# Hybrid decoder block on one Trainium2 core: first-row scores in one matmul for all heads, output-projection tiles held behind the last PV, merged high and low parts in the up projection

## The chip, the core and the metric

The kernel runs on one core of one Trainium2 chip. The metric is the device time of one execution in microseconds (us). A core has five engines that this text names as the profile does: PE (matrix multiply), PEld (its weight loads), DVE (elementwise), ACT (activation functions and copies), POOL (GpSimd; here it mostly issues adding DMAs) and SP (it only issues DMAs). Every engine works through its own queue in order. Matmul results go to PSUM, eight banks of 512 fp32 columns; the rest lies in SBUF.

## What is computed

A decoder block for 512 rows of width 1024, all in fp32; `x` is (1, 512, 1024):

```python
h = rmsnorm(x, norm_attn_g)
q, k, v, u_pool, u_gate = split(h @ w_in)        # 8 heads, two 64-wide score sets each, rope on q and k
w = softmax(s[:, :, 0]) - lam * softmax(s[:, :, 1])   # causal, in blocks of 128 rows
o = rmsnorm(w @ v, subln_g) * (1 - lam_init)
merged = sigmoid(g_A) * o + sigmoid(g_P) * pool(u_pool)   # gates u_gate, windows 2, 4, 8, 16
x = x + merged @ w_out
z = square(relu(rmsnorm(x, norm_mlp_g) @ w_up))  # 1024 -> 4096
x = x + z @ w_down                               # 4096 -> 1024
return rmsnorm(x, final_norm_g)
```

## The kernel before

**Numbers in two parts.** Each fp32 operand of a large matmul is split into a high part `hi` (rounded to fp32r) and a low part `lo` (the rest). A product is then three matmuls: hi by hi, hi by lo, lo by hi. A weight is split by `split_w`: ACT casts it (L112), DVE subtracts (L113).

**Attention (L372 to L545).** For each head `h`, `qk(h)` projects and rotates q and k, and `attn(h)` takes four row tiles `i`. The scores of a tile are, for each of the two sets `c`, two matmuls with the low and the high part of k (L406, L407). In the first tile, `i == 0`, heads 0 to 5 take another way (`whole`, L400): one matmul of 256 columns for each `c` gives both parts, and a DVE add (L402) and the following L408 bring them together. Heads 6 and 7 take the plain way with 128 columns. Then come softmax, transposes (L422), casts and subtracts of the weights `wt` (L424, L425), and PV (L430), twelve matmuls into bank 7. The row norm of the head's output follows: `sq`, a matmul with ones (`ss`, L445) into the same bank 7, and `rsqrt` on it: Ln, Exp, Square on ACT (L204, L205, L206), then two DVE instructions (L207, L208). L204 and L207 read `ss`, so bank 7 is free for the next head's PV only when L207 is done. Between these steps PE works on fillers: projections of gates and pools, dealt out by `LAG`. After every fifth filler, `gt` of a group of two heads goes through a sigmoid (L521), with an ACT table load ahead of it and one after it (L524), and `merge` makes the merged heads (L490 to L507), with matmuls `pp` (L499 to L503).

**Output projection (L622 to L656).** Its left half, `po0`, has a bank for each of four row tiles `t`. The weights come in four pieces `kk`; piece `kk` serves `k = 2kk, 2kk + 1`. The matmuls of `k = 4` are held behind the last PV (`state["pv"]`). The right half, `po1`, follows tile by tile. The last weight piece of `po1` reuses the buffer of the last piece of `po0`. A finished tile is added to x (`x1_add`, L604, and a Square, L578). Then each tile gets its row scale, is normed (`h2`, L655) and transposed (`h2T`, L663), and its parts are written to `gab` (L675, L676).

**MLP (L683 on).** The hidden width is done in four blocks `q`, each an `up(q)` and a `down(q)`. Each is a 2 by 2 block product with seven products instead of eight (forms A11, A12, S1, S2, S3, A22, S4 of the activations, kept in `gab` and `gss`). In `up`, a product is 48 matmuls of 256 columns: for each of two banks `i` and two halves `p`, four `k` with `hi` by the activations' high part (L802), four with `hi` by their low part (L805), four with `lo` by the high part (L808). A11, S2, S3 and A22 pile up in the same two banks `ma`, and after each of the first three its state is read: `keep` copies it (ACT, L830), `join` adds it (DVE, L834). `z_of` applies Relu and Square (L840, L841), `sub` and `zsplit` (L785, L783, L772, L775) make the forms of z for `down`, whose products are 24 matmuls of 512 columns (L895, L897, L898) and end in `to_x1` (L915). Weight forms for S1, S2 and A22 are made in place by adding DMAs (`plus`, L704, on POOL's queue), then split.

**Order.** Tile's scheduler moves instructions within each engine's queue by a time line of its own. `after(later, earlier)` gives it one more rule of order; it is not a wait of its own.

Of the kernel before, what the change touches and what calls it, by code (L numbers as in the profile page):

```python
# [51 lines left out]
def block_kernel(ctx, tc, xT, x_tok, gains, pos, consts, w_in, w_v, w_pool, w_out, w_up, w_dn, out):  # L52
# [334 lines left out]
    def attn(h, qs, kk):  # L387
        ks, kz = (kk[:, i] for i in range(2))
        wt = wt_all
        for i in range(NT):  # L390
            N = (i + 1) * P
            qsl = slice(i * P, i * P + P)
            pr = tmp(f"p{i}", f"p{h}_{i}", (P, 2, N), bufs=1)
            st = tmp("st", f"st{h}_{i}", (P, 6), bufs=3)
            whole = i == 0 and h < 6
            if whole:

                both = sbk(f"s{h}_0").rearrange("p (c k n) -> p c k n", c=2, k=2)
                for c in range(2):
                    T.matmul(both[:, c], lhsT=qs[:, c, qsl], rhs=kk[:, :, c, :P], start=c == 0, stop=True, skip_group_check=True)  # L400
                diag = mask[:, S - P :].rearrange("p (o n) -> p o n", o=1).to_broadcast([P, 2, P])
                V.tensor_tensor(out=pr, in0=both[:, :, 0], in1=diag, op=ALU.add)  # L402
            for c in range(2):
                if not whole:
                    s_ = sbk(f"s{h}_{i}_{c}")
                    T.matmul(s_[:, :N], lhsT=qs[:, c, qsl], rhs=ks[:, c, :N], start=True, stop=False)  # L406
                    T.matmul(s_[:, :N], lhsT=qs[:, c, qsl], rhs=kz[:, c, :N], start=False, stop=True)  # L407
# [12 lines left out]
            t_ = tbk(f"t{h}_{i}")  # L420
            for j in range(i + 1):
                T.transpose(out=t_[:, j * P : j * P + P], in_=pr[:, 0, j * P : j * P + P], identity=ident)  # L422
            tv = t_[:, :N].rearrange("p (j q) -> p j q", q=P)
            state["wt"] = A.copy(out=wt[:, 0, : i + 1, qsl], in_=tv)  # L424
            V.tensor_tensor(out=wt[:, 1, : i + 1, qsl], in0=tv, in1=f(wt)[:, 0, : i + 1, qsl], op=ALU.subtract)  # L425
# [181 lines left out]
    def forms_h2(forms, x):  # L607

        w, u, a11, a12 = (h_[:, i, :, x] for h_ in (hw, h2f) for i in range(2))
        for form in forms:  # L610
            ins = None
            if form in (S2, S4):
                ins = V.scalar_tensor_tensor(out=w, in0=w, scalar=-1.0, in1=a11 if form == S2 else a12, op0=ALU.mult, op1=ALU.subtract)
            elif form == S3:
                ins = V.tensor_tensor(out=u, in0=a11, in1=u, op=ALU.subtract)
            if form in (S3, S4):
                after(ins, state[form - 1])
            hi, lo = (g_[:, :, x] for g_ in gf[form])
            A.copy(out=hi, in_=u if form == S3 else w)
            state[form] = V.tensor_tensor(out=lo, in0=u if form == S3 else w, in1=f(hi), op=ALU.subtract)  # L620

    po = [bank(t, f"po0_{t}") for t in range(NT)]  # L622
    for kk in range(4):
        w = get_w(w_out[0, kk], f"o0_{kk}", V if kk else "dma", state["scaled"] if kk > 1 else None)
        for k in (2 * kk, 2 * kk + 1):
            for t in range(NT):
                m, _ = mm_rows(po[t], t, k, w, k == 0, k == NK - 1)
                if k == 4:
                    after(m, state["pv"])
    for t in range(NT):  # L630
        nc.sync.dma_start(out=x1[:, t, :], in_=x_tok[t])
# [5 lines left out]
    ws = []  # L637
    for kk in range(4):
        raw, hi, lo = load_w(w_out[1, kk], f"o1_{kk}")
        cast = split_w(raw, hi, lo, eng=V)  # L640
        ws.append((hi, lo))
    for ins in sq0:
        after(ins, cast)
    for t in range(NT):
        a_ = bank(4 + t, f"po1_{t}")
        for k in range(NK):
            m, end = mm_rows(a_, t, k, ws[k // 2], k == 0, k == NK - 1)
            if t > 1 and k == 0:
# [22 lines left out]
        if t == 3:  # L671
            forms_h2((S3,), slice(0, HS))
        for b in range(t // 2, 2):
            hi, lo = (gab[b][:, t // 2, i, :, sl] for i in range(2))
            A.copy(out=hi, in_=pv[b])  # L675
            part = V.tensor_tensor(out=lo, in0=pv[b], in1=f(hi), op=ALU.subtract)  # L676
# [12 lines left out]
    def weights(src, q, nm, order):  # L689
# [16 lines left out]
        def parts(rs, b, hold=None, add=None):  # L706
# [4 lines left out]
            for c in range(2):  # L711
# [51 lines left out]
    def halves(r):  # L763
        return [r[:, 2 * i : 2 * i + 2, :] for i in range(2)]

    def bank_view(pa):
        return [pa[i].rearrange("p (a t) -> p a t", a=2) for i in range(2)]

    def zsplit(q, form, r):

# [4 lines left out]
        lo = V.tensor_tensor(out=z[:, 1], in0=r, in1=f(z[:, 0]), op=ALU.subtract)  # L775
        if q == 0 and form == A11:
            after(lo, state["join"])

    def sub(o, x, y, neg=False):

        o, x, y = (R[i] for i in (o, x, y))
        if neg:
            V.scalar_tensor_tensor(out=o, in0=x, scalar=-1.0, in1=y, op0=ALU.mult, op1=ALU.subtract)  # L783
        else:
            V.tensor_tensor(out=o, in0=x, in1=y, op=ALU.subtract)  # L785

    def up(q):

        W = weights(w_up, q, "u", (A11, A12, S1, S2, S3, A22, S4) if q == 0 else (A11, S1, S2, S3, A22, A12, S4))

        def product(form, name, onto=None):
            w, pa = next(W), onto or [acc(f"u{name}{q}_{i}") for i in range(2)]
            rh, rl = gf[form]
            first.append(None)
            for i in range(2):
                hi, lo = w[i]
                for p in range(2):
                    begin = None
                    a_ = pa[i][:, p * HS : p * HS + HS]
# [26 lines left out]
            return pa  # L826

        def keep(pa, r):
            for a_, r_ in zip(bank_view(pa), halves(r)):
                state["keep"] = A.copy(out=r_, in_=a_)  # L830

        def join(pa, r, hold=None):
            for a_, r_ in zip(bank_view(pa), halves(r)):
                state["join"] = V.tensor_tensor(out=r_, in0=a_, in1=r_, op=ALU.add)  # L834
# [33 lines left out]
        zhi["z21"] = z_of(R[3], 1.0, ma)
# [183 lines left out]
```

## Time and profile before

| | |
|---|---|
| median of 3 runs | 671.15 us (670.84 to 671.32) |
| the profiled execution | 670.35 us |
| its span, first to last instruction | 668.6 us |
| granted PE clock | 0.998 |
| busy: PE, DVE, ACT, POOL | 99%, 80%, 70%, 14% |
| HBM read | 106.07 MB, 162 GB/s over the span |

The span is 1.75 us shorter than the time of the execution; what lies around it is outside the profile. Busy PE counts matmuls that overlap in a pipeline, so two starts are closer together than the length shown for one; the pace is read from starts. `out<-in` gives the tile written and those read. A bracket at the end of a row is idle time before it and what ended that. For windows, the columns are the stretch, its length, then busy time and number of instructions of each engine, granted clock, DMA share and GB/s.

### The profile page before, as it was taken

How to read it: one execution, taken by the hardware profiler on the slowest of the kernel's cores; microseconds unless marked ns; L12 is line 12 of the kernel's file. 1: busy time of each engine (PE TensorE's matmuls, PEld its weight loads, DVE VectorE, ACT ScalarE, POOL GpSimd, SP SyncE). 2: the span in 40 equal slices, each digit the busy share in tenths (PEclk: the TensorE clock that was granted, in tenths of full speed). 3: DMA queues.
4: the chain of work that ended last, by engine and by line, in shares of the span. 5: the costliest groups of instructions: out<-in, count | busy, mean ns of one | idle time of the engine just before them, and what ended most of it. 6: DMA issues, size and time to landing. Idle time of an engine off the chain costs nothing.

```text
span 668.6 us, 9970 instructions
## 1 busy us (share of the span) xinstructions
PE 659.8 (99%) x3668; PEld 576.7 (86%) x3668; DVE 531.6 (80%) x903; ACT 469.0 (70%) x756; POOL 92.5 (14%) x115
## 2 busy tenths in 40 slices
PE   9999999999999999999999999999999999999995
PEld 7888888888888888888789988999889998899884
DVE  6855977799879987895588998659993699657995
ACT  8465577988878689886577974368733695266875
POOL 3001110031113111300202030302102021210120
PEclk9999999999999999999999999999999999999999
DMA  8516465354445365554877495876949588584863
GB/s 319 166 61 179 125 151 139 69 146 96 120 109 140 113 140 112 126 186 161 269 203 137 156 235 166 184 212 139 243 168 205 173 179 257 121 200 136 211 126 127
DMA packets 32738, 108.83 MB, mean 163 GB/s; under 512 B 4016, under 2 KB 4912, under 8 KB 32688
## 3 DMA queue, kind: packets, MB, share of 16 engines
q0 software_dynamic: 10512, 38.28, 31.9%
q1 hardware_dynamic: 21744, 69.38, 29.6%
q8 instruction: 29, 0.48, 0.3%
q10 hardware_dynamic: 432, 0.52, 0.2%
q14 instruction: 21, 0.17, 0.1%
HBM read 106.07 MB, written 2.10 MB: 162 GB/s over the span
## 4 chain that ended last, share of the span: by engine, by line
PE 98%; DVE 0%; DMA 0%; ACT 0%; issue 0%; SPq 0%
PE um L805 8%; PE um L808 8%; PE um L802 8%; PE dm L897 8%; PE dm L895 8%; PE dm L898 8%; PE v L237 2%; PE o L430 2%; PE ga L137 2%; PE gp L133 2%; PE gp L134 2%; PE gp L137 2%; PE k L134 2%; PE ga L134 2%; PE k L133 2%; PE k L137 2%
## 5 line engine op out<-in xcount | busy, mean ns | idle before, releaser
L897 PE MATMUL dm<-wh_dt,z 128*128 128x512 f32 (+1 forms) x128 | 49.5, 386 | 0.0
L898 PE MATMUL dm<-wl_dt,z 128*128 128x512 f32 (+1 forms) x128 | 49.4, 386 | 0.0
L895 PE MATMUL dm<-wh_dt,z 128*128 128x512 f32 (+1 forms) x128 | 49.0, 387 | 0.0
L805 PE MATMUL um<-gss,wh_ut 128*128 128x256 f32 x192 | 48.2, 283 | 0.0
L802 PE MATMUL um<-gss,wh_ut 128*128 128x256 f32 x192 | 48.0, 283 | 0.0
L915 DVE TENSOR_TENSOR x<-x,dm 128x512 f32<-128x512 f32 x48 | 32.6, 682 | 16.7 <-PE dm L898 16.7
L112 ACT CAST wh_ut<-wga_uNone 128x1024 fp32r<-128x1024 f32 x24 | 24.9, 1052 | 29.1 <-PE dm L897 15.0
L112 ACT CAST wh_ub<-wr_u 128x1024 fp32r<-128x1024 f32 x24 | 25.1, 1050 | 25.6 <-PE um L805 11.1
L413 ACT ACTIVATE p<-p,st 128x128 f32<-128x128 f32 (+3 forms) x64 | 35.7, 559 | 5.9 <-DVE st L408 5.7
L113 DVE TENSOR_TENSOR wl_ut<-wga_uNone,wh_ut 128x1024 fp32r<-128x1024 f32 x24 | 29.0, 1222 | 12.6 <-ACT wh_ut L112 12.6
L897 PE MATMUL dm<-wh_db,z 128*128 128x512 f32 x96 | 37.2, 389 | 0.0
L898 PE MATMUL dm<-wl_db,z 128*128 128x512 f32 x96 | 37.2, 389 | 0.0
L805 PEld LDWEIGHTS um<-gss,wh_ut 128*128 128x128 f32 x192 | 36.9, 192 | 0.0
L802 PEld LDWEIGHTS um<-gss,wh_ut 128*128 128x128 f32 x192 | 36.8, 192 | 0.0
L895 PE MATMUL dm<-wh_db,z 128*128 128x512 f32 x96 | 35.7, 389 | 0.0
L113 DVE TENSOR_TENSOR wl_ub<-wr_u,wh_ub 128x1024 fp32r<-128x1024 f32 x24 | 29.1, 1220 | 8.3 <-ACT wh_ub L112 8.3
L704 POOL DMA_DIRECT2D wga_dNone<-w_dn x16 | 13.9, 871 | 152.2 <-DVE wl_dt L113 152.2
L775 DVE TENSOR_TENSOR z<-rawz,z 128x1024 fp32r<-128x1024 f32 x28 | 33.6, 1219 | 1.5 <-ACT z L772 1.4
L112 ACT CAST wh_dt<-wga_dNone 128x1024 fp32r<-128x1024 f32 x24 | 24.8, 1047 | 11.6 <-issue 7.5
L805 PE MATMUL um<-gab,wh_ub 128*128 128x256 f32 x128 | 32.5, 283 | 0.0
L802 PE MATMUL um<-gab,wh_ub 128*128 128x256 f32 x128 | 32.4, 283 | 0.0
L704 POOL DMA_DIRECT2D wga_uNone<-w_up x18 | 15.6, 864 | 115.6 <-DVE wl_ut L113 99.2
(326 smaller groups left out, 2185.3 us busy)
## 6 DMA issues: line engine op xcount, KB each, us to landing
wr_u<-w_up SPq DMA_DIRECT2D x24, 512.0 KB, 5.5
wr_d<-w_dn SPq DMA_DIRECT2D x24, 512.0 KB, 4.1
wga_uNone<-w_up POOLq DMA_DIRECT2D x18, 512.0 KB, 7.1
wga_dNone<-w_dn POOLq DMA_DIRECT2D x16, 512.0 KB, 5.5
wr_k<-w_in SPq DMA_DIRECT2D x8, 512.0 KB, 3.3
wr_ga<-w_in SPq DMA_DIRECT2D x8, 512.0 KB, 3.4
wr_gp<-w_in SPq DMA_DIRECT2D x8, 512.0 KB, 4.1
wl_ga<-w_in POOLq DMA_DIRECT2D x8, 512.0 KB, 5.6
```

Of the source, the lines that this page charges most:

```text
L112: ins = A.copy(out=hi[:, sl], in_=raw[:, sl])
L113: state["low"] = (eng or G).tensor_tensor(out=lo[:, sl], in0=raw[:, sl], in1=f(hi)[:, sl], op=ALU.subtract)
L134: T.matmul(acc, lhsT=hi[:, c], rhs=rl[k], start=False, stop=False)
L137: T.matmul(acc, lhsT=lo[:, c], rhs=rh[:, k, :], start=False, stop=k == NK - 1)
L413: A.activation(out=pr[:, c, :N], in_=pr[:, c, :N], func=AF.Exp, scale=-1.0, bias=st[:, c : c + 1], accum_out=st[:, 2 + c : 3 + c])
L775: lo = V.tensor_tensor(out=z[:, 1], in0=r, in1=f(z[:, 0]), op=ALU.subtract)
L802: m = T.matmul(a_, lhsT=hi[:, c], rhs=rh[:, k, :], start=p + k == 0 and onto is None, stop=False, skip_group_check=True)
L805: T.matmul(a_, lhsT=hi[:, c], rhs=rl[:, k, :], start=False, stop=False, skip_group_check=True)
L808: m = T.matmul(a_, lhsT=lo[:, c], rhs=rh[:, k, :], start=False, stop=k == 3, skip_group_check=True)
L895: m = T.matmul(a_, lhsT=zh, rhs=hi[:, sl], start=p == 0 and start, stop=False, skip_group_check=True)
L897: T.matmul(a_, lhsT=zl, rhs=hi[:, sl], start=False, stop=False, skip_group_check=True)
L898: end = T.matmul(a_, lhsT=zh, rhs=lo[:, sl], start=False, stop=p == 3, skip_group_check=True)
```

## The change

Four edits:

1. `whole` holds for all eight heads: heads 6 and 7 take the way of L400 too.
2. The matmuls of `k = 0` for tiles 0 and 2 of `po0` are held behind the last PV as well; those of `k = 4` of `po1`'s tile 1 are held behind the end of `po0`'s tile 3.
3. The last weight piece of `po1` is cast and subtracted in two halves of 512 columns.
4. In `up(q)` for q = 1, 2, 3 the products A11, S2, S3 and A22 are `wide`: the activations' high and low parts lie side by side (`gab`, `gss` are laid out `[..., 4, 2, HS]`), and one matmul of 512 columns does what L802 and L805 did. The `lo` matmuls stay at 256 columns. The result has its two halves in one bank, and a product has four banks instead of two. So `keep` becomes an ACT copy and a DVE add for each of four banks, `join` two DVE adds for each, and A22's `z_of` goes through `keep` first. The rotation of banks is set for each q. In `up(3)`, the weight of A12 is loaded and split ahead of A22's. Some `after` rules are added for weight casts and for `sub`.

```diff
-            whole = i == 0 and h < 6
+            whole = i == 0 and h < 8
...
-                if k == 4:
+                if k == 4 or k == 0 and t % 2 == 0:
                     after(m, state["pv"])
...
-        cast = split_w(raw, hi, lo, eng=V)
+        for sl in (slice(0, 512), slice(512, 1024)) if kk == 3 else (slice(0, 1024),):
+            cast = split_w(raw, hi, lo, sl, eng=V)
...
+            elif t == 1 and k == 4:
+                after(m, state["po0", NT - 1])
...
+            if nm == "u" and q == 3 and form == A22:
+                b21 = parts(raw(2), "b21")
...
+                    if wide:
+                        ab = pa[2 * i + p]
+                        a_ = ab[:, :HS]
...
+                        if wide:
+                            m = T.matmul(ab, lhsT=hi[:, c], rhs=both[:, k].rearrange("p a t -> p (a t)"), start=k == 0 and onto is None, stop=False, skip_group_check=True)
+                            first[-1] = first[-1] or m
+                            continue
...
         def keep(pa, r):
+            if len(pa) == 4:
+                for i, ab in enumerate(map(split_view, pa)):
+                    state["kept", i] = A.copy(out=r[:, i, :], in_=ab[:, 1])
+                    V.tensor_tensor(out=r[:, i, :], in0=ab[:, 0], in1=r[:, i, :], op=ALU.add)
+                return
...
         def join(pa, r, hold=None):
+            if len(pa) == 4:
+                for i, ab in enumerate(map(split_view, pa)):
+                    for j in range(2):
+                        ins = V.tensor_tensor(out=r[:, i, :], in0=ab[:, j], in1=r[:, i, :], op=ALU.add)
+                        state["joined", i] = ins
+                return
...
+            if pa and len(pa) == 4:
+                keep(pa, r)
+                pa = None
...
+        wide = q > 0
+        if wide:
+            x, y, z = ((0, 1), (6, 7), (4, 5)) if q % 2 else ((4, 5), (6, 7), (0, 1))
+            acc.ids, acc.n = x + y + z + x + y + x + z, 0
+        ma = product(A11, "m1", wide=wide)
...
+        product(S2, "m6", onto=ma, wide=wide)
...
+        product(S3, "m7", onto=ma, wide=wide)
...
+        product(A22, "m4", onto=ma, wide=wide)
```

With the edits the scheduler also places other instructions anew. Three places follow.

The first is ACT's queue at the row norm of head 6, near the end of attention: `y_2499` (in the change `y_2497`) is head 6's norm, `ss` its sum, `t_3` the last score tile of head 7, and `g` the gates of the last group. Before:

```order
L112 CAST wh_o_3_3081<-wr_o_3_3079 128x1024
L424 CAST wt<-t_2_2701 128x3x128
L204 ACTIVATE y_2499<-ss_2497,eps 128x512
L205 ACTIVATE y_2499<-y_2499 128x512
L206 ACTIVATE sqo_2489<-y_2499 128x512
L424 CAST wt<-t_3_2723 128x4x128
L521 ACT_TABLE_LOAD
L521 ACTIVATE g_2761<-g_2761 128x2048
L524 ACT_TABLE_LOAD
```

In the change:

```order
L112 CAST wh_o_3_3077<-wr_o_3_3075 128x1024
L204 ACTIVATE y_2497<-ss_2495,eps 128x512
L424 CAST wt<-t_3_2719 128x4x128
L521 ACT_TABLE_LOAD
L521 ACTIVATE g_2757<-g_2757 128x2048
L524 ACT_TABLE_LOAD
L205 ACTIVATE y_2497<-y_2497 128x512
L206 ACTIVATE sqo_2487<-y_2497 128x512
```

The cast of `t_3`, both table loads and the sigmoid moved from behind L206 to between L204 and L205. On PE, 4 transposes and 26 matmuls of 512 columns stand between `ss` of head 6 and the PV of head 7 before; in the change it is 4 transposes and 18 matmuls.

The second is PE's queue where `po0` ends and `po1` first needs its last weight piece; `po_0_2984` to `po_3_2987` (in the change `po_0_2980` to `po_3_2983`) are the tiles of `po0`, the others those of `po1`, and `wl_o_3_3152` (`wl_o_3_3148`) is the low part of the last piece. Before:

```order
L600 MATMUL po_3_2987<-wh_o_3_3081,vl 128x512
L600 MATMUL po_1_3204<-wh_o_1_3139,vl 128x512
L598 MATMUL po_1_3204<-wh_o_2_3145,vh 128x512
L599 MATMUL po_1_3204<-wl_o_2_3146,vh 128x512
L600 MATMUL po_1_3204<-wh_o_2_3145,vl 128x512
L598 MATMUL po_1_3204<-wh_o_2_3145,vh 128x512
L599 MATMUL po_1_3204<-wl_o_2_3146,vh 128x512
L600 MATMUL po_1_3204<-wh_o_2_3145,vl 128x512
L598 MATMUL po_0_3155<-wh_o_3_3151,vh 128x512
L598 MATMUL po_1_3204<-wh_o_3_3151,vh 128x512
L599 MATMUL po_0_3155<-wl_o_3_3152,vh 128x512
```

In the change (two rows more at the head):

```order
L600 MATMUL po_0_2980<-wh_o_3_3077,vl 128x512
L600 MATMUL po_1_2981<-wh_o_3_3077,vl 128x512
L600 MATMUL po_2_2982<-wh_o_3_3077,vl 128x512
L600 MATMUL po_3_2983<-wh_o_3_3077,vl 128x512
L598 MATMUL po_1_3202<-wh_o_2_3141,vh 128x512
L599 MATMUL po_1_3202<-wl_o_2_3142,vh 128x512
L600 MATMUL po_1_3202<-wh_o_2_3141,vl 128x512
L598 MATMUL po_1_3202<-wh_o_2_3141,vh 128x512
L599 MATMUL po_1_3202<-wl_o_2_3142,vh 128x512
L600 MATMUL po_1_3202<-wh_o_2_3141,vl 128x512
L598 MATMUL po_0_3153<-wh_o_3_3147,vh 128x512
L598 MATMUL po_1_3202<-wh_o_3_3147,vh 128x512
```

The four tiles of `po0` now end in four successive matmuls, 12 matmuls ahead of the first use of the last low part; before, tiles 0, 1 and 2 ended 8, 6 and 3 matmuls ahead of tile 3's end, the first row shown. On DVE the four `x1_add` of these tiles stand ahead of the last piece's subtract in both programs.

The third is DVE's queue at the parts of the first two normed tiles; `h2T_0_3237` (`h2T_0_3235`) is the second tile's transpose for A11, whose parts go to `gab_2978` (`gab_2974`), and `h` is a normed tile. Before:

```order
L676 TENSOR_TENSOR gab_2978<-h2T_0_3188,gab_2978 128x4x128
L676 TENSOR_TENSOR gab_2979<-h2T_1_3193,gab_2979 128x4x128
L676 TENSOR_TENSOR gab_2978<-h2T_0_3237,gab_2978 128x4x128
L591 SCALAR_TENSOR_TENSOR st_2983<-st_2983 128x1
L676 TENSOR_TENSOR gab_2979<-h2T_1_3242,gab_2979 128x4x128
L604 TENSOR_TENSOR x_2974<-po_3_3305,x_2974 128x512
L592 SCALAR_TENSOR_TENSOR st_2983<-st_2983 128x1
L655 SCALAR_TENSOR_TENSOR h_2976<-x_2974,st_2983,rawz 128x1024
```

In the change:

```order
L679 TENSOR_TENSOR gab_2974<-h2T_0_3186,gab_2974 128x4x128
L679 TENSOR_TENSOR gab_2975<-h2T_1_3191,gab_2975 128x4x128
L591 SCALAR_TENSOR_TENSOR st_2979<-st_2979 128x1
L592 SCALAR_TENSOR_TENSOR st_2979<-st_2979 128x1
L658 SCALAR_TENSOR_TENSOR h_2972<-x_2970,st_2979,rawz 128x1024
L679 TENSOR_TENSOR gab_2974<-h2T_0_3235,gab_2974 128x4x128
L604 TENSOR_TENSOR x_2970<-po_3_3303,x_2970 128x512
L679 TENSOR_TENSOR gab_2975<-h2T_1_3240,gab_2975 128x4x128
```

The normed third tile (L658) moved ahead of the second tile's first subtract. On PE, seven matmuls of `po1` stand between the second tile's transposes and the first matmul of `up(0)` before, and three in the change.

More of the change, by code (lines that the diff above doesn't have):

```diff
@@ L560, in block_kernel @@
     h2f = zf("h2f", F32)
-    gab = [big.tile([P, j, 2, 4, HS], F32R, tag=t_, name=f"gab{j}") for j, t_ in ((1, "s1a"), (2, "s4"))]
-    gss = [big.tile([P, 2, 2, 4, HS], F32R, tag=f"s{i}", name=f"gss{i}") for i in (2, 3)]
+    gab = [big.tile([P, j, 4, 2, HS], F32R, tag=t_, name=f"gab{j}") for j, t_ in ((1, "s1a"), (2, "s4"))]
+    gss = [big.tile([P, 2, 4, 2, HS], F32R, tag=f"s{i}", name=f"gss{i}") for i in (2, 3)]
     gf = {}
     for form, g_, j in ((A11, gab[0], 0), (A12, gab[1], 0), (A22, gab[1], 1), (S1, gss[0], 0), (S2, gss[0], 1), (S3, gss[1], 0), (S4, gss[1], 1)):
-        gf[form] = (g_[:, j, 0], g_[:, j, 1])
+        gf[form] = (g_[:, j, :, 0], g_[:, j, :, 1], g_[:, j])
     rawz = bk.tile([P, 5, 4, HS], F32, name="rawz")
@@ L617, in forms_h2 @@
                 after(ins, state[form - 1])
-            hi, lo = (g_[:, :, x] for g_ in gf[form])
+            hi, lo = (g_[:, :, x] for g_ in gf[form][:2])
             A.copy(out=hi, in_=u if form == S3 else w)
@@ L626, in block_kernel @@
             for t in range(NT):
-                m, _ = mm_rows(po[t], t, k, w, k == 0, k == NK - 1)
-                if k == 4:
+                m, state["po0", t] = mm_rows(po[t], t, k, w, k == 0, k == NK - 1)
+                if k == 4 or k == 0 and t % 2 == 0:
                     after(m, state["pv"])
@@ L673, in block_kernel @@
         for b in range(t // 2, 2):
-            hi, lo = (gab[b][:, t // 2, i, :, sl] for i in range(2))
+            hi, lo = (gab[b][:, t // 2, :, i, sl] for i in range(2))
             A.copy(out=hi, in_=pv[b])
@@ L726, in parts @@
                     after(state["low"], state["h2", 0])
-                if early and b == f"t{A22}":
-                    after(cast, state["keep"])
+                if b == f"t{A22}" and nm == "u":
+                    after(cast, state["keep"] if early else state["kept", 2 * c + 1])
+                    if q == 3 and c:
+                        after(cast, state["joined", 0])
+                if b == "b22" and nm == "u" and q == 3 and c == 0:
+                    after(cast, state["joined", 1])
                 out_.append((hi, lo))
@@ L747, in weights @@
             elif form == A12:
-                yield parts(raw(2), "b21", zhi[q, A11] if nm == "d" and q else None)
+                yield b21 if nm == "u" and q == 3 else parts(raw(2), "b21", zhi[q, A11] if nm == "d" and q else None)
             elif form == S4:
@@ L764, in halves, with split_view @@
         return [r[:, 2 * i : 2 * i + 2, :] for i in range(2)]
+    def split_view(b_):
+        return b_.rearrange("p (a t) -> p a t", a=2)
     def bank_view(pa):
-        return [pa[i].rearrange("p (a t) -> p a t", a=2) for i in range(2)]
+        return [split_view(pa[i]) for i in range(2)]
     def zsplit(q, form, r):
@@ L774, in zsplit @@
             after(hi, state[S4])
-        lo = V.tensor_tensor(out=z[:, 1], in0=r, in1=f(z[:, 0]), op=ALU.subtract)
+        lo = state["zlow", form] = V.tensor_tensor(out=z[:, 1], in0=r, in1=f(z[:, 0]), op=ALU.subtract)
         if q == 0 and form == A11:
@@ L782, in sub @@
         if neg:
-            V.scalar_tensor_tensor(out=o, in0=x, scalar=-1.0, in1=y, op0=ALU.mult, op1=ALU.subtract)
+            ins = V.scalar_tensor_tensor(out=o, in0=x, scalar=-1.0, in1=y, op0=ALU.mult, op1=ALU.subtract)
+            after(ins, state["zlow", A11])
         else:
@@ L789, in up, with product @@
         W = weights(w_up, q, "u", (A11, A12, S1, S2, S3, A22, S4) if q == 0 else (A11, S1, S2, S3, A22, A12, S4))
-        def product(form, name, onto=None):
-            w, pa = next(W), onto or [acc(f"u{name}{q}_{i}") for i in range(2)]
-            rh, rl = gf[form]
+        def product(form, name, onto=None, wide=False):
+            w, pa = next(W), onto or [acc(f"u{name}{q}_{i}") for i in range(4 if wide else 2)]
+            rh, rl, both = gf[form]
             first.append(None)
@@ L842, in z_of @@
             return ins
-        ma = product(A11, "m1")
+        wide = q > 0
[3 more added lines that the diff above has]
+        ma = product(A11, "m1", wide=wide)
         keep(ma, R[0])
@@ L858, in up @@
         keep(mc, R[2])
-        product(S2, "m6", onto=ma)
+        product(S2, "m6", onto=ma, wide=wide)
         keep(ma, R[1])
-        product(S3, "m7", onto=ma)
+        product(S3, "m7", onto=ma, wide=wide)
         join(ma, R[2])
@@ L864, in up @@
         z_of(R[2], -1.0)
-        product(A22, "m4", onto=ma)
+        product(A22, "m4", onto=ma, wide=wide)
         if q == 0:
```

3 lines of the change are left out of this document (2 added, 1 removed).

## The prediction

> **What bounds the kernel now.** I read the page's totals and chain first, then PE's waits, then its time line at the one wait of any size.
>
> ```profile
> span 668.6 us, 9970 instructions
> PE 659.8 (99%) x3668; PEld 576.7 (86%) x3668; DVE 531.6 (80%) x903; ACT 469.0 (70%) x756; POOL 92.5 (14%) x115
> PE 98%; DVE 0%; DMA 0%; ACT 0%; issue 0%; SPq 0%
> ```
>
> PE carries 98% of the chain that ended last. Its list of waits over the whole span has two rows:
>
> ```profile
> PE warm L172 <- POOL eps L163: 1.1, 1, 1.1
> PE po L599 <- DVE wl_o L113: 0.4, 1, 0.4
> ```
>
> One lies at the start; the other is the last weight piece of the output projection:
>
> ```profile
> 329.50 0.61 PE L598 MATMUL po<-wh_o,vh 128*128 128x512 f32 x2
> 330.48 0.50 PE L599 MATMUL po<-wl_o,vh 128*128 128x512 f32 x1 [0.36 <-DVE wl_o L113]
> 330.82 0.39 PE L600 MATMUL po<-wh_o,vl 128*128 128x512 f32 x1
> ```
>
> So from 5 us on PE is the bound in every stage. Two things follow. PE work taken out comes off the time in full. And any wait put into PE's queue adds to it in full, because PE has no idle time later in which to win it back. The pace of PE comes from two windows: `down(1)` without its last product, and that product with `up(2)`:
>
> ```profile
> 466.09:498.75 32.66, 32.66 (x146) 27.03 (x145) 31.75 (x34) 19.62 (x21) 1.73 (x2) 1.00 0.74 208
> 498.75:544.55 45.80, 45.80 (x362) 44.81 (x360) 28.94 (x29) 28.04 (x37) 8.76 (x10) 1.00 0.75 175
> ```
>
> The first holds six `down` products, 144 matmuls of 512 columns, and two that overlap its edges: 32.66/144 = 0.227 us each. The second holds the seventh (24 of those, 5.45 us) and the 336 narrow ones of `up`: 40.35/336 = 0.120 us. The granted clock is 1.00 in both.
>
> **Edit 4 on PE: -2.5 us.** A wide matmul takes 0.227 where two narrow ones took 0.240. That is 0.013 for each of 16 pairs, four products and three blocks: 192 x 0.013 = 2.5 us (2.3 to 2.8 by the rounding). It is not half the work: the columns streamed stay the same, only a matmul's fixed part goes.
>
> **Edit 1: -0.44 us.** One plain pair of head 6 and its follower:
>
> ```profile
> 242.92 0.22 PE L406 MATMUL s<-kk,qs 128*128 128x128 f32 x1
> 242.98 0.27 PE L407 MATMUL s<-kk,qs 128*128 128x128 f32 x1
> 243.09 0.68 PE L137 MATMUL q<-xh,wl_q 128*128 128x512 f32 x2
> ```
>
> The pair takes 0.17, and its follower's 0.68 for two is 0.06 longer than two at that pace (0.227 + 0.39). Four pairs cost 0.92, four matmuls of 256 columns 0.48. The DVE add that comes with each head (0.41, a row below) lies beside PE's fillers; without that cover it is 0.8 at most.
>
> **Edit 2 and the new order at head 7's PV: +3.35 us.** Bank 7 holds `ss` of head 6 until L207, then the PV of head 7. From PE's, ACT's and DVE's time lines:
>
> ```profile
> 296.10 0.39 PE L445 MATMUL ss<-sqp,onesr 128*128 128x512 f32 x1
> 298.17 0.60 PE L422 MATMUL t<-ident,p 128*128 128x128 f32 x4
> 298.52 0.48 PE L598 MATMUL po<-wh_o,vh 128*128 128x512 f32 x1
> 302.79 0.75 PE L430 MATMUL o<-wt,vh 128*128 128x512 f32 x4
> ```
>
> ```profile
> 296.52 0.69 ACT L204 ACTIVATE y<-ss,eps 128x512 f32<-128x512 f32 x1
> 297.25 0.64 ACT L205 ACTIVATE y<-y 128x512 f32<-128x512 f32 x1
> 297.91 0.63 ACT L206 ACTIVATE sqo<-y 128x512 f32<-128x512 f32 x1
> 298.80 0.59 ACT L424 CAST wt<-t 128x512 fp32r<-128x512 f32 x1 [0.25 <-PE t L422]
> 299.41 1.28 ACT L521 ACT_TABLE_LOAD   x1
> 300.70 1.92 ACT L521 ACTIVATE g<-g 128x2048 f32<-128x2048 f32 x1
> 302.63 1.28 ACT L524 ACT_TABLE_LOAD   x1
> ```
>
> ```profile
> 298.58 0.69 DVE L207 SCALAR_TENSOR_TENSOR sqo<-ss,sqo 128x512 f32<-128x512 f32 x1
> ```
>
> Before, L207 ends at 299.27 and PV starts at 302.79: 3.5 us to spare. The change takes this from both sides. PE has 18 matmuls between instead of 26: 0.23 for `ss`, 0.35 for the transposes (298.17 to 298.52), 4.27 for the 18 (298.52 to 302.79), so PV comes up 4.85 after `ss` starts. ACT now has the cast, two loads and the sigmoid between Ln and Exp, and its queue is strictly in order: 0.42 to the start of L204, 0.69, 0.59, 1.28, 1.92, 1.28, 0.64 for L205, 0.67 from L206's start to L207's, 0.69 for L207. That is 8.2, and the wait 8.2 - 4.85 = 3.35 (3.0 if neighbours on ACT overlap by 0.1). Queued behind the waiting PV on PE are all matmuls of the output projection; nothing can pass. The eight matmuls of `po0` that head 6's `ss` had behind it before now stand ahead of it.
>
> The page "ScalarE: Activation LUTs" of the Trainium skill, section "What ACT_TABLE_LOAD costs", puts a drain of about 1.38 us behind each load. The row speaks against it: the sigmoid starts 1.29 after the load ahead of it. By the page two drains would add 2.8 us, and the time would be 677.3.
>
> Holding tiles 0 and 2 itself is free: their `k = 0` stands behind PV before, too. SP issues one load of `po1` ahead of x's rows now; those are first read at 326 us.
>
> **Edit 3: +0.25 us.** What counts is what ends last ahead of the subtract:
>
> ```profile
> 325.88 0.39 PE L600 MATMUL po<-wh_o,vl 128*128 128x512 f32 x1
> 326.30 2.51 DVE L604 TENSOR_TENSOR x<-po,x 128x512 f32<-128x512 f32 x4 [2.41 <-PE po L600]
> L113 DVE TENSOR_TENSOR wl_v<-wr_v,wh_v 128x512 fp32r<-128x512 f32 x16 | 10.9, 687 | 2.8 <-ACT wh_v L112 2.6
> ```
>
> The first row is tile 0's end. Now that it is 12 matmuls ahead of the first use (2.72 us, before 18), the four adds of DVE are last, not the cast: 0.42 from that row's start to the adds, 2.45 for them, 0.69 for a half subtract, 0.05 to release PE, 3.6 in all, so PE waits 0.9. Before it lost 0.52 ahead of L599 (330.48 - 329.73 - 0.23) and 0.11 behind it. Bounds 0 to 0.4 more; the halves only keep it from being 0.5 worse.
>
> **The order at the first `up` product: +1.5 us.** Rows of PE and DVE, and the group of normed tiles:
>
> ```profile
> 343.07 1.03 PE L663 MATMUL h2T<-ident,h 128*128 128x128 f32 x8
> 343.87 0.48 PE L600 MATMUL po<-wh_o,vl 128*128 128x512 f32 x1
> 345.66 0.34 PE L805 MATMUL um<-gab,wh_ub 128*128 128x256 f32 x1
> ```
>
> ```profile
> 343.68 1.88 DVE L676 TENSOR_TENSOR gab<-h2T,gab 128x512 fp32r<-128x512 f32 x3
> 345.48 0.21 DVE L591 SCALAR_TENSOR_TENSOR st<-st 128x1 f32<-128x1 f32 x1
> ```
>
> ```profile
> L655 DVE SCALAR_TENSOR_TENSOR h<-x,st,rawz 128x1024 f32<-128x1024 f32 x4 | 5.1, 1284 | 0.1
> ```
>
> The third of those subtracts ends at 345.56, 0.1 ahead of L805: no slack. Four fewer matmuls ahead of it bring PE 0.9 earlier (0.8 with the first one's longer start), and the normed tile, 1.28, now stands ahead of that subtract. Part of it fits while DVE waits for the cast, so 0.8 to 1.9; I take 1.5.
>
> **Edit 4 on DVE and ACT: +1.2 us.** The prices are those of nearest shape:
>
> ```profile
> L402 DVE TENSOR_TENSOR p<-s,mask 128x256 f32<-128x256 f32 x6 | 2.5, 415 | 0.3 <-PE s L400 0.3
> L834 DVE TENSOR_TENSOR rawz<-um,rawz 128x512 f32<-128x512 f32 x24 | 16.4, 687 | 8.1 <-PE um L808 8.0
> 472.78 2.36 DVE L775 TENSOR_TENSOR z<-rawz,z 128x1024 fp32r<-128x1024 f32 x2
> 477.45 0.39 PE L897 MATMUL dm<-wh_db,z 128*128 128x512 f32 x1
> ```
>
> A block gains 12 adds for `keep` and 8 for `join`, and loses two of L834: 20 x 0.41 - 1.4 = 6.8 us of DVE. DVE was busy 28.94 of 45.80 in the one window and 31.75 of 32.66 in the other. So `up` has 16.9 free and `down` 0.9: what `up` doesn't absorb goes straight into the z parts that `down` waits for. The closest there is A12's, done at 474.0 and used at 477.45, 3.45 to spare. A22's path grows most: four copies on ACT, four adds (1.6), and only then Relu. PSUM is rather easier, as each of four banks is free a quarter product after its last matmul. I take 0.4 a block, between 0 and 1.3. The added casts' rules, A12's weight ahead of A22's in `up(3)` and the wider layout change no count and lie on the same queues; POOL's order is as before.
>
> **The sum.** -2.5 - 0.44 + 3.35 + 0.25 + 1.5 + 1.2 = +3.4. The profiled execution took 670.35, of which 668.6 are span; it becomes 673.7. The median of the runs is 0.8 above it, 671.15, and becomes 674.5.
>
> **The rivals.** *The savings win.* The waits at PV, at the last piece and at the first `up` stay under 2 us together, because ACT takes the sigmoid before `ss` arrives. Then 671.15 - 2.9 + 1.5 = 669.7. It decides at 2.9 us of waits. For it speaks that all but the last-piece wait rest on queue order; against it, that the Ln ahead of the load can't run before `ss`, so the 4.5 us of loads and sigmoid always lie between. Chance 0.08.
>
> *DVE becomes the bound in `up`.* Each block waits 1.3 or more. For it: 31.75 of 32.66. Against: 16.9 free in `up`. Time 674.5 + 2.7 = 677.2. Chance 0.12.
>
> *PE falls to half pace behind the wait.* At the start of the program it does run so:
>
> ```profile
> 1.10:4.30 3.20, 3.16 (x15) 3.16 (x16) 0.49 (x1) 1.79 (x2) 3.00 (x8) 1.00 0.68 205
> ```
>
> 15 matmuls in 3.20 us are 0.213 each, where the eight transposes of the same width at 343.07 take 0.10 each. If 3.2 us at half pace follow the PV wait, 1.6 go: 676.1. Against: the start followed no work at all, the wait follows 300 us of it. The page "TensorE: Matmul & The Clock Gate" of the Trainium skill, Part 1, has the clock halved after a whole idle window of about 3.4 us; this wait is just below that, and no trace here shows one. Chance 0.10.
>
> **The numbers.** My forecast, 674.5, has 0.70, with 672.5 to 676.3 as its own range. The range 671.9 to 677.3 takes in both slow rivals' times and the low ends of the unknown waits. A measurement here tells 0.2%, 1.3 us, from no change: faster is below 669.8, slower above 672.5. Faster 0.06, same 0.09, slower 0.85.
>
> **What would show it.** PE's waits in the changed profile should hold one of some 3 us at L430, released by L207; one near 0.9 at the last piece; one of 1 to 2 at the first `um`; and DVE waits of tenths in `um` or `dm`. Starts of wide matmuls should lie 0.227 apart. I am wrong if PE's row at L430 shows under 1 us, or if `up` itself takes longer than 40.35 a block.

## The result and the profile after

The changed kernel takes 678.9 us, the median of five runs (677.19 to 680.45); a sixth run of 2438.58 us was disturbed as a whole and is left out, as are one of 2342.75 us of the last mended kernel and one of 1103.12 us of the kernel before, both further down. The kernel before took 671.2 us in six runs on the same chip. The ratio is 1.0115, 95% interval 1.0102 to 1.0128: slower by 7.7 us, where 3.4 was forecast, and outside the range. The runs lie 3.3 us apart, where those of the kernel before lie 1.1 apart. The profiled execution took 680.19, 9.8 more than that of before; its span is 678.4.

From the page of the changed kernel, the span, the busy times and the granted PE clock in 40 slices:

```profile
span 678.4 us, 9663 instructions
...
PE 663.2 (98%) x3472; PEld 569.1 (84%) x3472; DVE 548.9 (81%) x960; ACT 471.0 (69%) x781; POOL 92.5 (14%) x115
...
PEclk9999999999999999998999999999999999999999
```

PE has 196 matmuls fewer and is busy 3.4 us longer. That alone says that it runs slower somewhere; the 8 in the clock's row says where, a little before the middle. PE's list of waits, but for the one of 1.1 at the start:

```profile
PE o L430 <- DVE sqo L207: 2.8, 1, 2.8
PE um L823 <- ACT gab L678: 1.4, 1, 1.4
PE um L826 <- DVE gab L679: 1.4, 1, 1.4
PE po L599 <- DVE wl_o L113: 0.7, 1, 0.7
PE um L820 <- DVE rawz L862: 0.4, 1, 0.4
```

The first, the third and the fourth stand where the forecast put a wait (L826 is L805 of before). The second was not foreseen. Around the two places, in stretches of 3.41 us, the column ahead of the last two is the granted clock:

```profile
303.22:306.63 3.41, 0.59 (x4) 0.17 (x2) 2.15 (x4) 2.55 (x4) 0.00 (x0) 1.00 1.03 419
306.63:310.04 3.41, 3.41 (x11) 3.12 (x12) 1.40 (x2) 0.00 (x0) 1.28 (x1) 0.50 0.73 298
310.04:313.45 3.41, 3.41 (x18) 2.83 (x17) 2.41 (x4) 2.61 (x5) 0.00 (x0) 1.00 0.00 0
...
351.01:354.42 3.41, 0.90 (x4) 0.26 (x2) 3.34 (x7) 2.23 (x6) 0.00 (x0) 1.00 0.66 223
354.42:357.83 3.41, 3.12 (x14) 3.12 (x15) 2.02 (x6) 3.06 (x8) 0.00 (x0) 0.50 0.21 84
```

Twice the clock is 0.50 for exactly 3.41 us, each time right behind a stretch of the same length in which PE was busy for less than 1 us. The two starts, 306.63 and 354.42, are 47.79 apart, 14 such lengths: the clock is granted on a fixed grid. Each drop costs at most half of 3.41, 1.7 us. On PE's time line at PV:

```profile
303.40 0.39 PE L600 MATMUL po<-wh_o,vl 128*128 128x512 f32 x1
306.61 1.43 PE L430 MATMUL o<-wt,vh 128*128 128x512 f32 x4 [2.82 <-DVE sqo L207]
...
310.13 0.44 PE L598 MATMUL po<-wh_o,vh 128*128 128x512 f32 x1
```

PV starts 3.21 after the matmul ahead of it instead of 0.23: 2.98 late. Its twelve matmuls then take 3.52. On ACT and DVE, three steps of the chain that PV waits for, the Ln (L204), the Exp behind the second table load (L205), and L207, which releases PV:

```profile
298.83 0.69 ACT L204 ACTIVATE y<-ss,eps 128x512 f32<-128x512 f32 x1 [0.99 <-PE ss L445]
304.54 0.63 ACT L205 ACTIVATE y<-y 128x512 f32<-128x512 f32 x1
305.86 0.69 DVE L207 SCALAR_TENSOR_TENSOR sqo<-ss,sqo 128x512 f32<-128x512 f32 x1 [1.19 <-ACT sqo L206]
```

`ss` starts at 298.40 and L207 ends at 306.55, 8.15 later.

At the first `up` product there are two waits with one matmul between, as PE's, ACT's and DVE's time lines show:

```profile
351.13 0.40 PE L600 MATMUL po<-wh_o,vl 128*128 128x512 f32 x1
352.98 0.38 PE L823 MATMUL um<-gab,wh_ub 128*128 128x256 f32 x1 [1.45 <-ACT gab L678]
354.71 0.58 PE L826 MATMUL um<-gab,wh_ub 128*128 128x256 f32 x1 [1.35 <-DVE gab L679]
```

```profile
351.85 0.59 ACT L683 COPY h2f<-h2T 128x512 f32<-128x512 f32 x1 [0.66 <-DVE gab L679]
352.33 1.08 ACT L678 CAST gab<-h2T 128x512 fp32r<-128x512 f32 x2
```

```profile
348.86 2.35 DVE L113 TENSOR_TENSOR wl_ub<-wr_u,wh_ub 128x1024 fp32r<-128x1024 f32 x2
351.13 1.29 DVE L679 TENSOR_TENSOR gab<-h2T,gab 128x512 fp32r<-128x512 f32 x2
...
352.77 1.28 DVE L658 SCALAR_TENSOR_TENSOR h<-x,st,rawz 128x1024 f32<-128x1024 f32 x1
353.97 0.68 DVE L679 TENSOR_TENSOR gab<-h2T,gab 128x512 fp32r<-128x512 f32 x1
```

Two weight subtracts hold up the first tile's gab subtracts on DVE. ACT's copy of `h2f` waits for those, and the second tile's casts stand behind that copy. The second tile's subtract then stands behind a normed tile. Each of L823 and L826 starts 1.62 late, 3.24 in all.

The rest is small. Down(1) without its last product, and that product with up(2):

```profile
475.84:508.60 32.76, 32.76 (x147) 26.96 (x145) 32.48 (x33) 20.36 (x23) 1.73 (x2) 1.00 0.67 188
508.60:554.45 45.85, 45.40 (x298) 41.45 (x296) 34.02 (x47) 28.16 (x43) 8.76 (x10) 1.00 0.75 184
```

Before, they took 32.66 and 45.80: in this block edit 4 brings nothing. PE starts 0.61 late at L820, behind an add of `join` (L862) that stands behind a weight subtract on DVE:

```profile
534.97 0.41 DVE L862 TENSOR_TENSOR rawz<-um,rawz 128x256 f32<-128x256 f32 x1
535.30 1.22 DVE L113 TENSOR_TENSOR wl_ut<-wga_uNone,wh_ut 128x1024 fp32r<-128x1024 f32 x1
536.43 0.75 DVE L862 TENSOR_TENSOR rawz<-um,rawz 128x256 f32<-128x256 f32 x2
```

### The profile page after: what moved, and what is told of

Its sections match the earlier page's. It is cut to its first block, busy times and chain, and to the rows that moved or that the text cites. A ratio compares the mean times of both kernels' runs of the same rounds, so it can differ in the third digit from the quotient of the medians.

```text
span 678.4 us, 9663 instructions
## 1 busy us (share of the span) xinstructions
PE 663.2 (98%) x3472; PEld 569.1 (84%) x3472; DVE 548.9 (81%) x960; ACT 471.0 (69%) x781; POOL 92.5 (14%) x115
## 4 chain that ended last, share of the span: by engine, by line
PE 73%; issue 13%; DMA 9%; DVE 3%; ACT 2%; POOL 0%; POOLq 0%; ACTq 0%
PE dm L937 4%; PE dm L936 4%; PE dm L934 4%; PE um L829 4%; DMA wga_uNone<-w_up 3%; PE um L826 3%; PE um L823 3%; PE um L820 3%; PE o L430 2%; DMA wga_dNone<-w_dn 2%; PE v L237 2%; PE gp L134 2%; PE ga L137 2%; PE gp L137 2%; PE gp L133 2%
## 5 line engine op out<-in xcount | busy, mean ns | idle before, releaser
L784 ACT CAST z<-rawz 128x1024 fp32r<-128x1024 f32 x28 | 28.4, 1048 | 14.7 <-DVE rawz L795 13.0
L829 PE MATMUL um<-gss,wl_ut 128*128 128x256 f32 x192 | 30.7, 282 | 0.0
L113 DVE TENSOR_TENSOR wl_dt<-wga_dNone,wh_dt 128x1024 fp32r<-128x1024 f32 x24 | 28.8, 1219 | 1.2 <-ACT wh_dt L112 1.2
L829 PEld LDWEIGHTS um<-gss,wl_ut 128*128 128x128 f32 x192 | 27.9, 190 | 2.0
L937 PEld LDWEIGHTS dm<-wl_dt,z 128*128 128x128 f32 x128 | 24.0, 188 | 4.9
L936 PEld LDWEIGHTS dm<-wh_dt,z 128*128 128x128 f32 x128 | 24.0, 188 | 4.8
```

The lines of the kernel that those rows point to most:

```text
L113: state["low"] = (eng or G).tensor_tensor(out=lo[:, sl], in0=raw[:, sl], in1=f(hi)[:, sl], op=ALU.subtract)
L829: m = T.matmul(a_, lhsT=lo[:, c], rhs=rh[:, k, :], start=False, stop=k == 3, skip_group_check=True)
L936: T.matmul(a_, lhsT=zl, rhs=hi[:, sl], start=False, stop=False, skip_group_check=True)
L937: end = T.matmul(a_, lhsT=zh, rhs=lo[:, sl], start=False, stop=p == 3, skip_group_check=True)
```

## The experiments

Theory A: a wait of PE costs its length, and a grid step of 3.41 us in which PE was mostly idle halves the clock of the next, up to 1.7 us more. Both waits come from the scheduler's new order. Rival B: the drops have nothing to do with the waits. Rival C: part of the loss lies in the blocks, that is, in edit 4.

**Edit 1 undone.**

```diff
-            whole = i == 0 and h < 8
+            whole = i == 0 and h < 6
```

> The changed kernel (678.9 us) without edit 1: heads 6 and 7 take the plain way of scores again. In the scheduler's order this alone puts the sigmoid of the last group back behind L206 of head 6, so bank 7 is free before PV; tile 1's four h2T transposes have 4 instead of 3 matmuls behind them ahead of the first um, but the normed tile still comes early on DVE. Theory A (a wait costs its length, and one near 3 us also costs 3.4 us at half clock behind it, 1.7 us): the PV wait of 2.98 and its 1.7 go, edit 1's 0.44 is lost, 674.6; if the shorter waits at the first um (some 1.5 to 2 instead of 3.2) no longer bring the second drop, 671.6 to 672.9. Theory B (the drops of the clock have nothing to do with the waits): 676.3, with the granted clock at half for 3.4 us near 306 us all the same.

Measured 669.93 us (11 runs, 669.02 to 670.38), ratio to before 0.9982 (0.9973 to 0.9990). PE's list of waits holds only the one at the start:

```profile
PE warm L172 <- POOL eps L163: 1.1, 1, 1.1
```

The clock is full from 7.36 to 666.13 us, which is 193 steps. B would have a drop near 306 us; it falls. More went than expected: at the first `um` PE is 0.18 late in place of 3.24, and so the second drop had no cause left. One edit whose own price by the forecast is a gain of 0.44 takes 9 us with it, through the order that the scheduler made of it.

**Edit 3 undone.**

```diff
-        for sl in (slice(0, 512), slice(512, 1024)) if kk == 3 else (slice(0, 1024),):
-            cast = split_w(raw, hi, lo, sl, eng=V)
+        cast = split_w(raw, hi, lo, eng=V)
```

> The changed kernel without edit 3: the last weight piece is cast and subtracted whole again. The scheduler's order then has 5 matmuls instead of 3 between tile 1's transposes and the first um, and all four gab subtracts ahead of the third normed tile; the PV wait is as in the change. Theory A: the PV wait (2.8) and its drop stay; the two waits of 1.6 at the first um shrink to less than 1 together and the drop behind them goes, -2.2 to -3.2 and -1.7; the whole piece costs 0.5: 674.5 to 675.5. Theory B: -2.2 to -3.2 and +0.5 alone, 676.2 to 677.2, and a drop near 354 us stays.

Measured 675.85 (6 runs), ratio 1.0077 (1.0059 to 1.0095). The waits:

```profile
PE o L430 <- DVE sqo L207: 2.8, 1, 2.8
PE po L599 <- DVE wl_o L113: 1.1, 1, 1.1
PE um L825 <- DVE gab L678: 0.5, 1, 0.5
```

As A has it, the drop behind PV stays (the clock is 0.50 from 306.21 to 309.62) and the one behind the first `um` is gone. The runs differ in the mean clock: 674.06 at 0.998, the value of a run without a drop; 675.81 twice at 0.996, the profiled run with its one drop among them; 675.88 and 676.52 at 0.994; 678.55 at 0.993. Only one run of each kernel was traced, and the mean is a rough sign: it also counts the half clock behind the last matmul, 2.0 to 5.3 us in the traces. If the waits are the same each time, the program has a drop only in some runs. That fits a grid whose phase against the program differs: the profiled runs first have full clock at 4.29 (before), 5.84 (here) and 7.36 us (edit 1 undone). The last weight piece, whole, makes PE 1.32 late at L599 instead of 0.85.

**Edit 4 alone** (the kernel before with it).

> The kernel before (671.2 us) with edit 4 alone (wide products in up(1) to up(3), the wider layout of gab and gss). The order at the PV of head 7 and at the first um is that of before. As the trace of the change has it (blocks 0.71, -0.15 and 0.85 us shorter, the tail 0.5 longer): -0.9, 670.3. By the forecast's PE price alone (-2.5, waits on DVE and ACT hidden): 668.7. By the rival in which DVE becomes the bound in up (more than 1.3 a block of waits): 672.6 or more.

Measured 670.01 (11 runs), ratio 0.9987 (0.9978 to 0.9995): 1.0 us faster. The two windows as above:

```profile
466.27:499.02 32.75, 32.75 (x146) 26.96 (x145) 32.47 (x33) 20.34 (x23) 1.73 (x2) 1.00 0.68 188
499.02:544.30 45.28, 45.28 (x297) 41.42 (x296) 33.89 (x47) 28.16 (x43) 8.76 (x10) 1.00 0.78 188
```

The three blocks are 0.69, 0.43 and 0.61 shorter (1.73 in all), and the tail behind up(3) 0.5 longer, late weights of the last `down`. C falls: edit 4 is a gain. The forecast's sum for it, -1.3, lies inside the interval, -0.3 to -1.5, but both of its terms were too large. The wide matmuls of S2, S3 and A22 start mostly 0.233 apart where 0.227 was taken, and the waits of 0.4 a block aren't there. The expectation's 0.85 for the third block of the change was a misreading: it is 0.62.

**Edits 1 to 3, without 4.**

> The kernel before with edits 1, 2 and 3, without edit 4. The order at head 7's PV and at the first um is word for word that of the change. Theory A (all of the loss comes from these places, edit 4 is a gain of its own of about 1): waits of 3.0 and 3.2 and up to two drops of 1.7, less edit 1's 0.44: 676.7 to 680, median about 679.5, with the same spread over some 3 us as the change. Theory C (part of the loss is in the blocks): 677 or less, a gain of over 2 against the change.

Measured 680.6 (4 runs, 679.3 to 681.22), ratio 1.0141 (1.0126 to 1.0156). It has the waits of 2.8 at L430 and of 0.9 and 1.4 at the first `um`, and both drops. (Its profiled run also waits 1.3 us for operands of v near the start, as the change's does not.) So all of the loss, and more, is in edits 1 to 3.

**Edit 1 alone.**

> The kernel before with edit 1 alone. In the scheduler's order the sigmoid comes ahead of head 6's Exp as in the change, but PE has 39 matmuls and 4 transposes between ss and PV: 0.23 + 0.35 + 39 x 0.227 = 9.4 us, more than the 8.2 of the chain on ACT. So no wait at PV, and -0.44: 670.6 against 671.0. Against it: if edit 1 alone made the wait, it would be 674 or more.

Measured 675.73 (5 runs), ratio 1.0070 (1.0057 to 1.0082). I expected 670.6. There is no wait at PV, as expected, but a place that I hadn't looked at:

```profile
PE po L599 <- DVE wl_o L113: 1.2, 1, 1.2
PE po L598 <- ACT wh_o L112: 1.1, 1, 1.1
```

```profile
331.03:334.44 3.41, 1.12 (x4) 0.64 (x5) 3.34 (x11) 3.38 (x9) 1.74 (x3) 1.00 1.01 350
334.44:337.85 3.41, 3.41 (x10) 2.63 (x9) 0.91 (x3) 0.85 (x4) 1.53 (x2) 0.50 1.01 268
```

The cast of the last weight piece waits for the last L600 of `po0`, which reads the buffer that the piece goes into. In this order the last four matmuls of `po0` stand right ahead of the first use of the piece. So both of its parts come late, 2.6 in all. The two waits, two matmuls apart, leave PE busy for 1.12 of a step, and the next is at half clock. One of the five runs does not fit: 675.73 has the mean clock of a run without a drop, 0.997, and is no shorter than the four at 0.994. It was not traced, and this stays open. Edit 1 alone brings the new order on ACT (table load, sigmoid and table load between Ln and Exp), but PV stands 39 matmuls behind `ss` and not 18. The wait at PV is there without edit 3 and without edit 4, so it takes edit 2, which moves PV forward; no run has edits 1 and 2 alone. The forecast had the mechanism right and gave the new order to the wrong edit.

**The sigmoid behind head 6's norm** (the changed kernel with one rule of order).

```diff
-        A.activation(out=t, in_=dst, func=AF.Square, scale=1.0 / math.sqrt(n))
+        state["norm"] = A.activation(out=t, in_=dst, func=AF.Square, scale=1.0 / math.sqrt(n))
...
         rsqrt(y, ss, sq, P)
+        state["norm", h] = state["norm"]
...
                         if g == 3:
                             after(sg, state["wt"])
+                            after(sg, state["norm", 6])
```

> The changed kernel with one rule of order more: the sigmoid of the last group (L521) comes behind the Square (L206) of head 6's norm. ACT's queue is then Ln, cast, Exp, Square, table load, sigmoid. PE still has 22 matmuls and transposes between ss and PV, 4.85 us, and L207 should end some 4.3 after ss: no wait at L430. The order at the first um becomes that with all four gab subtracts ahead of the third normed tile, with 4 matmuls between. Theory A: -2.98 and -1.7 at PV; at the first um -2 or so, and its drop goes: 670.3; with that drop still there 672. Theory B: the drops stay, 674 to 676.

Measured 669.66 (11 runs), ratio 0.9980 (0.9971 to 0.9989). On ACT's, DVE's and PE's time lines:

```profile
299.43 0.65 ACT L205 ACTIVATE y<-y 128x512 f32<-128x512 f32 x1
300.10 0.63 ACT L206 ACTIVATE sqo<-y 128x512 f32<-128x512 f32 x1
300.75 1.28 ACT L522 ACT_TABLE_LOAD   x1
```

```profile
300.77 0.69 DVE L207 SCALAR_TENSOR_TENSOR sqo<-ss,sqo 128x512 f32<-128x512 f32 x1 [0.20 <-ACT sqo L206]
```

```profile
303.16 0.75 PE L430 MATMUL o<-wt,vh 128*128 128x512 f32 x4
```

L207 ends at 301.46, 1.7 ahead of PV, and PV's four matmuls take 0.75 where they took 1.43. The scheduler also makes a better order at the first `um`, so this run doesn't tell the two places apart. But for the one at the start, two waits are left, both in up(2), at L822: PE starts 0.68 and 0.63 late there, behind adds on DVE.

**That, and the weight subtracts in up(2) behind the wide joins.**

```diff
-                if b == "b22" and nm == "u" and q == 3 and c == 0:
+                if b == "b22" and nm == "u" and q > 1 and c == 0:
                     after(cast, state["joined", 1])
```

> The changed kernel with the sigmoid behind head 6's Square, as in the run before this, and one rule more: in up(2) too the cast of S4's first weight half comes behind the last wide join, as the change has it for up(3). That takes two weight subtracts of 1.2 us from between the adds that free up(2)'s banks. There the trace of the last run has PE late by 0.68 and 0.63 at L822. Theory A (those adds behind a weight subtract are the whole of it): 669.7 - 1.2 = 668.5. Theory B (the weight subtracts are only late elsewhere, at S4's product or in down(2)): 669.4 to 669.9.

Measured 669.0 (median of five runs, 668.61 to 669.22), ratio 0.9970 (0.9958 to 0.9982), 2.0 us faster than the kernel before. This version beats both. L822's two late starts went from 0.68 and 0.63 to one of 0.26. The gain of 0.6 between the two versions lies inside the intervals of their ratios and isn't shown by them alone.

**A wait made to size.** Three kernels hold the kernel before at one place: two, three or five DVE adds into scratch stand ahead of the last weight piece's subtract.

```diff
+        if kk == 3:
+            dums = [V.tensor_tensor(out=R[0][:, 2:4, :].rearrange("p a t -> p (a t)"), in0=x1[:, 3, 0:512], in1=x1[:, 3, 0:512], op=ALU.add) for _ in range(3)]
...
+        if kk == 3:
+            after(state["low"], dums[-1])
```

> The kernel before with two more DVE adds between the last add of po0 and the subtract of the last weight piece: PE some 1.8 late at L599, about 1.6 of it idle. Theory A with a bound of about half a step: at most 1.6 of 3.41 us idle in a step, no drop, 672.4 in every run and clock 0.997 to 0.998. If the bound is lower than 1.6 of 3.41, some runs show a drop and take 674.

> The kernel before with three more DVE adds of 0.61 (into scratch) between the last add of po0 and the subtract of the last weight piece, so that PE waits longer at L599 (0.52 late before, some 2.4 to 2.7 late now); nothing else waits. Theory A (the clock is granted anew on a fixed 3.41 us grid, and a step of it that was mostly idle halves the next): 671.0 + 1.9 to 2.2 in runs where the wait falls across two steps, and up to 1.7 more where one step holds most of it: 673 to 675, spread over more than 1 us, the clock 0.995 or so in the slower ones. Theory B (drops have nothing to do with waits): 673.0 in every run, clock 0.998.

> As before, with five such adds: PE some 3.6 to 4 late at L599. Theory A: with a wait longer than one step of the grid, a step that is mostly idle is met in nearly every run: 671.0 + 3.3 + 1.7 = 676, few runs without the drop. Theory B: 674.3 in every run.

| adds | PE idle at L599 | runs | their times | drop in the profiled run |
|---|---|---|---|---|
| 2 | 1.5 | 10 | 671.59 to 672.68 | none |
| 3 | 2.3 | 4 | 672.45; 674.98, 675.00, 675.22 | one step |
| 5 | 3.8 | 4 | 677.88 to 678.38 | two steps |

The step with the wait and the one behind it, for two adds:

```profile
329.80:333.21 3.41, 1.96 (x9) 1.31 (x8) 2.81 (x11) 3.41 (x10) 1.13 (x2) 1.00 0.95 199
333.21:336.62 3.41, 3.41 (x17) 2.82 (x16) 1.40 (x3) 2.12 (x9) 0.00 (x0) 1.00 1.05 223
```

For three:

```profile
331.19:334.60 3.41, 1.09 (x6) 0.90 (x6) 2.47 (x11) 2.57 (x7) 0.86 (x1) 1.00 1.02 213
334.60:338.01 3.41, 3.41 (x10) 2.65 (x9) 1.39 (x3) 1.42 (x5) 0.00 (x0) 0.50 1.05 228
```

For five:

```profile
329.86:333.27 3.41, 0.56 (x3) 0.14 (x1) 3.34 (x13) 3.01 (x9) 0.86 (x1) 1.00 1.05 222
333.27:336.69 3.42, 2.49 (x6) 2.01 (x7) 0.88 (x1) 0.00 (x0) 0.00 (x0) 0.50 1.06 211
336.69:340.10 3.41, 3.41 (x10) 2.64 (x9) 1.85 (x5) 1.93 (x6) 0.00 (x0) 0.50 1.03 256
```

This shows A's second half: between the first two PE's order is the same up to this place, only the length of the one wait differs, and the drop comes with it. PE starts 0.87 later at L599 (2.48 and 1.61 late), and the medians, 672.22 and 674.99, lie 2.8 apart; the rest is near the price of one drop. With three adds one run of four, not traced, took 672.45: there the clock's mean is 0.997, not 0.994 or 0.995, as it would be if the wait fell across two steps. With five, two steps are lost where I expected one, and two waits of 0.6 and 0.4 in up(0) come on top: 678.1 and not 676.

PE busy 1.96 of a step brought no drop, 1.12 (edit 1 alone) did. Two more places in the traces narrow the bound. The first is the second drop of edits 1 to 3 without 4:

```profile
352.48:355.89 3.41, 1.48 (x10) 1.28 (x11) 3.34 (x7) 2.61 (x6) 0.00 (x0) 1.00 0.80 304
355.89:359.30 3.41, 3.41 (x19) 3.41 (x18) 2.01 (x5) 3.21 (x9) 0.00 (x0) 0.50 0.00 0
```

The other is the step in which PE's work ends, here with five adds:

```profile
667.78:671.19 3.41, 1.63 (x14) 1.43 (x12) 2.04 (x8) 2.74 (x13) 0.00 (x0) 1.00 0.13 49
671.19:674.61 3.42, 0.00 (x0) 0.00 (x0) 1.13 (x3) 1.25 (x3) 0.00 (x0) 1.00 0.76 290
```

By the busy time that the profile shows, the bound lies between 1.48 and 1.63 of 3.41. The last step of other kernels agrees: 1.68 (edit 1 undone) and 1.78 (before) leave the next at full clock, and 1.45 (edit 1 alone) is followed by half.

## Why the prediction was wrong

**PE falls to half pace: the step that failed.** The forecast knew this and priced it rightly, at 1.6: the twelve PV matmuls took 3.52 instead of some 1.9, and the second drop cost 1.41, which is what `up(0)` is longer beyond L826's wait. It failed in the chance, 0.10, and in the reason: "the start followed no work at all, the wait follows 300 us of it". What counts is one step of 3.41 us, not the 300 us ahead. The rule cited there, of the page "TensorE: Matmul & The Clock Gate" of the Trainium skill, Part 1, asks for a whole idle window of about 3.4 us. The measured step differs: 2.3 us of one wait were enough, or two of 1.1 and 1.2; what decides is whether PE was busy for more than some 1.5 of the 3.41. The same section has a free-running activity window, and the grid of the traces agrees with that. The forecast also allowed for one drop and there were two: 3.1 us of the 6.5 by which the profiled execution, 680.19, lies above the 673.7 forecast for it.

**The first `up` product, +1.5: mis-sized.** It cost 3.24. The forecast weighed DVE's subtract for L826 against PE and left out L823 ahead of it, which needs ACT's cast. That cast came late for a reason that stands in the queues' order too: a copy that waited for DVE stood ahead of it on ACT, and two weight subtracts ahead of that on DVE. The upper end, 1.9, didn't hold it. And the first wait together with the second is what made the second drop: neither is near 3.4 by itself, and each is about as long as the wait of 1.5 that made no drop with two adds.

**Head 7's PV, +3.35: right.** 2.98 measured, at the line and with the releaser named. The chain from `ss` to L207 took 8.15 where the sum had 8.2, with no drain behind a table load, as the row of before said; the difference is that PE reached PV 0.38 later than taken. What was wrong is the heading: the order on ACT comes from edit 1, and edit 2 only brings PV into it.

**The last weight piece, +0.25: right.** L599 is 0.85 late and the next matmul 0.11, 0.96 where it was 0.64 before: +0.32. That the halves keep it from being 0.5 worse holds as well: undoing them made L599 1.32 late.

**Edit 1, -0.44: right, as far as the trace shows it.** No run has it by itself, since every kernel with it has another order. But up to head 7's PV both programs do the same matmuls, save four fewer with edit 1, and PV starts 3.82 later in the change. Of that 2.98 is the wait, 0.89 the start of the program and 0.38 late starts of PE behind DVE's L488 near 299 us, which leaves -0.43.

**Edit 4, -2.5 and +1.2: sum near, terms wrong.** Alone it brings -1.0 (interval -0.3 to -1.5), by -1.7 in the blocks and +0.5 in the tail. In the change the blocks bring 0.71, -0.15 and 0.62, up(2) losing 0.61 to a wait for L862, the kind of wait that the forecast named. The rival in which DVE becomes the bound in `up` has its mechanism here, at half the price and in one block of three.

**The sum as it came out**, between the two profiled executions, by PE's starts: 2.98 + 0.32 + 3.24 for the waits, 1.65 + 1.41 for the two drops, -1.18 for the blocks, +0.53 for the tail, -0.43 for edit 1, +0.38 for the late starts near 299 us and +0.89 at the start of the program make 9.79 of the 9.84. The last term belongs to the traced runs and not to the change: PE had full clock from 6.26 us in the one and from 4.29 in the other. Without the two drops the median would have been near 675.8, an estimate from 678.9 and 3.1, which is inside the range.

## What to carry to other kernels

On a kernel that PE bounds, look not only for how long a new wait is but for how much PE works within each 3.41 us around it: two short waits near each other cost like one long one, and a run-to-run spread that grew from 1 to 3 us went with it here. A small edit in a program whose order a scheduler makes is priced by the order that comes out, so read the queues of every engine at every place where PE was close to waiting, for the first operand it needs as well as the last. When an edit has made things worse, one rule of order at the place of the wait can be worth more than the edit: here it turned +7.7 us into -1.4, and a second rule brought the kernel to -2.0.

## What the runs showed of the hardware that was not expected

- The granted clock changes only at multiples of 3.41 us from one another: the stretches at full clock were 300.37, 44.37 and 317.44 us in the change and 658.77 in the kernel with edit 1 undone, that is 88, 13, 93 and 193 steps. The phase differs between the traced runs. Where a wait is about 2.3 us long, the times of the other runs fit a drop in most of them and none in some.
- A step at half clock in which PE was busy 2.49 of 3.41 us was followed by another at half (five adds), and so was one of 2.81 at the start of the program (edit 1 undone, by the pace of its matmuls). Steps at half with 3.07 (edit 4 alone, at the start) and 3.12 (the second drop of the change) were followed by full clock. If work at half pace counts half, these are 1.25, 1.41, 1.54 and 1.56, and one bound near 1.5 would serve for all steps. That fits; no run was made to test it.
- The wide matmuls of A11, whose banks are fresh, start 0.227 apart, as those of `down` do, until near the end of the product; those of S2, S3 and A22, which add to the same banks, mostly 0.233. The cause was not tried and stays open.
